# A hybrid DeltaNet and neighbourhood-attention layer: scores three gate tiles later, an empty step in the preparation, scan loads in another order

## The chip, the cores and the metric

The kernel runs on one NeuronCore of a Trainium2 chip. The core has a matrix engine (TensorE, PE in the profile; its weight loads are shown as PEld), a vector engine (VectorE, DVE), a scalar engine (ScalarE, ACT), GpSimd (POOL), and SyncE (SP), whose queue issues nearly all transfers between HBM and the on-chip memory SBUF. TensorE writes its sums into banks of PSUM, from which the others copy. The metric is the time of one execution on the device, in microseconds (us), as the median of several runs.

## What is computed

One layer on 1024 latent tokens of width 1024 with 256 context tokens ahead of them, so 1280 in all, in 32-bit floats. Cut to what matters here:

```
px = modulate(rms_norm(x), sh1, sc1) @ w_in          # and the same for the context
group A (4 heads of 128), forward and backward, chunk by chunk:
    q, k, v = silu(short_conv(...)); q, k normalised; decay g, gate beta
    m    = strict_lower((k*beta) k^T * decay);  u, w = solve(1 + m, ...)
    v_new = u - w S;  o = (q e^g) S + (q k^T * decay) v_new;  S = S e^g_last + k_dec^T v_new
    o = rms_norm(o_forward + o_backward) * silu(z)
group B (8 heads of 64): softmax over an 8 x 16 window of a 16 x 64 grid and all context keys
x = x + g1 * (concat(A, B) @ w_out)
x = x + g2 * swiglu(modulate(rms_norm(x), sh2, sc2))
```

The two directions of group A scan ten chunks of 128 tokens each: two of context, eight of latents. The solve is done by blocks of 32, all of it before the scans, since it doesn't depend on the state S.

## The kernel before

All matrix products are made from a high and a low part of each operand (three products for one), with sums in PSUM.

**Projection jobs.** A list of jobs runs over the columns of `w_in`: blocks k0 to k3, z1 (one half of the gate z), nk0 to nk3 with nv0 among them, q0 to q3, nq0 to nq3, v0, nv1, v1 to v3, and z0, the other half of the gate. A block holds 128 columns and is computed in eight steps over the depth (L405); a wide job holds 256 columns and is computed in ten tiles of 128 tokens (nv0, nv1) or eight (z0; only latents), 24 matmuls to a tile (L595). The job nv1 is the one that the loop calls `values`. A job's weights are loaded, cast to a high part on ACT and subtracted to a low part on POOL while the job before it runs. For a wide job they come in two halves through one raw buffer, so the second half is asked for when the first has been split (L586 to L588). After a block of kind q, k or v comes its convolution on DVE (L457, L461); later its transposes (L527) and stores.

**Background.** A generator `bg` is advanced by one call after each of a block's eight steps and by two after each tile of a wide job. From job nk0 on it first makes the inverses of the 32 x 32 blocks, then the preparations; what is left is drained ahead of v3. Another (`bg2`) makes the modulation.

**Preparation.** Ten preparations, each for a forward and a backward chunk at once. Each is a generator of seven calls: (1) decay terms on POOL, copies to `fx` on ACT; (2) decay matmuls (L967, L968), exponent on ACT, the mask product of `kk` on DVE (L974), the block inverses into `y` on POOL (L977), `at` on DVE; (3) block products `kk` x `fx` (L986) and their copy (L989); (4 to 6) three rounds of products (L997), each copied into `y` by DVE (forward, L999) and ACT (backward, L1000); (7) the end, which puts the stores of `y` on a list. Stores of `y` and `at` are issued on SP one or two calls later (L1009). Two preparations may be alive; a second starts once the first has had three calls. `y` has two buffers, used in turn, and the products two PSUM banks. Preparations 2 to 9 wait until the jobs of kind q are finished, which is at job nq2.

**Value windows.** After nv1's tiles the program asks SP for 64 copies inside HBM (L1107), which lay the values out by window (`vw_d`).

**Attention.** Group B is a generator (`fill`) that is advanced between other work. Its first call, ahead of v3's matmuls, asks for the first queries, keys, biases and values (L260 to L283). There are 32 blocks of two heads each; a block takes two calls: scores (L303), the softmax on DVE and ACT (L305 to L309), transposes (L314) with copies (L317), the product with the values (L324). In z0 it is called after each of the eight tiles. The rest is called beside the scans, `PACE` times to each call of a scan generator, and what is left after them.

**Scans.** `scan(d, c)` does one chunk of one direction in four calls (three in each direction's first chunk, which has no state): state times `kT` (L1195), state times `qT` (L1205), `y` times the residual (L1214), `at` times the new values (L1226), `kt` times the decayed values into the next state (L1231). `load(d, c, near)` asks SP for a chunk's tiles (all at L1164), for the next chunk while one is scanned. A chunk that the other direction needs next is loaded once.

The order of instructions on an engine starts from the order of the program, but a planner at build time moves instructions whose operands it expects later behind others; so order on PE and SP need not be the program's. The first part of the kernel, up to job k1, is excepted from it.

Of the kernel before, what the change touches and what calls it, by code (L numbers as in the profile page):

```python
# [51 lines left out]
NCONST = 4 * 128 + 4 * 32  # L52
WIN = (256, 0)
CTX = {256: slice(0, 256), 0: slice(384, 640)}
PACE = 0.63
AHEAD = {(1, 0): (3,), (1, 1): (3, 4), (2, 0): (4, 5), (2, 1): (5, 6, 7), (3, 0): (6, 7)}
ORDER = [list(range(NCH)), [1, 0] + list(range(9, 1, -1))]

# [30 lines left out]
def hybrid(ctx, tc, a, dbg):  # L89
# [50 lines left out]
    v_d = dram.tile([T, 512], F32, name="v_d", tag="v_d")  # L140
# [34 lines left out]
    bg = Background()  # L175
# [199 lines left out]
    with ExitStack() as bs:  # L375
# [541 lines left out]
        def preps():  # L917

            first_half.close()
            with ExitStack() as gs:  # L920
                pk = pools(gs, "pk", "left")
                shift(gs, "ppad", "left", 64)
                pp = pools(gs, "pp", "left")

                def work(name, bufs=2, dt=F32):
                    return (pk if name == "kk" else pp).tile([128, 4, 128], dt, name=name, tag=name, bufs=bufs)

                fxs = [work(f"fx{d}", 1) for d in range(2)]
                ys = [[work(f"y{d}{i}", 1) for d in range(2)] for i in range(2)]
                for t in fxs + ys[0] + ys[1]:  # L930
                    pool.memset(t, 0.0)
                q32 = [slice(b * 32, b * 32 + 32) for b in range(4)]

                def fetch(i):

                    got = []
                    for d in range(2):
                        c = ORDER[d][i]
                        kk, xc = work("kk", 6), pp.tile([128, 2, 4, 32], F32, name="xc", tag="xc", bufs=4)
                        sp.dma_start(kk, kk_d[:, c])  # L940
                        sp.dma_start(xc, x_d[:, d, :, c * 4:c * 4 + 4])
                        at = None
                        if c >= 2:
                            at = work("at", 4)
                            sp.dma_start(at, qk_d[:, c - 2])
                        got.append((d, c, kk, xc, at))
                    return i, got

                def prep(i, got):
                    y = ys[i % 2]  # L950
                    rgs = []
                    for d, c, kk, xc, at in got:
                        mle = M[C_LE + d].rearrange("p (o i) -> p o i", o=1).to_broadcast([128, 4, 128])
                        for gg in (GH, GL):
                            rg = work("rg", 4, F32R)
                            g = gg.bitcast(F32)[:, d, c].rearrange("p (h o) -> p h o", o=1).to_broadcast([128, 4, 128])
                            pool.tensor_tensor(rg, g, mle, OP.mult)
                            rgs.append(rg)
                    for d, c, kk, xc, at in got:
                        for q in q32:  # L960
                            act.copy(fxs[d][q, :, q], xc[q, 1])
                    yield 1
                    es = []
                    for d, c, kk, xc, at in got:
                        p = bank("pr")
                        for j in range(2):
                            pe.matmul(p, mr[:, d], fl(rgs[2 * d + j]), start=j == 0, stop=False)  # L967
                        pe.matmul(p, mr[:, 4], mneg[:, d].rearrange("p (o i) -> p o i", o=1).to_broadcast(  # L968
                            [128, 4, 128]), start=False, stop=True)
                        e = work("e", 2)  # L970
                        act.activation(fl(e), p, AF.Exp)
                        es.append(e)
                    for (d, c, kk, xc, at), e in zip(got, es):
                        dve.tensor_tensor(kk, kk, e, OP.mult)  # L974
                    for (d, c, kk, xc, at), e in zip(got, es):
                        for q in q32:
                            pool.tensor_copy(y[d][q, :, q], xc[q, 0])  # L977
                        if at is not None:
                            dve.tensor_tensor(at, at, e, OP.mult)
                            stores.append((at_d[d, c - 2], at, tick[0] + 2))  # L980
                    yield 1
                    ps = []
                    for d, c, kk, xc, at in got:
                        p = bank("pr")
                        for h in range(4):
                            pe.matmul(p[:, hs[h]], kk[:, h], fxs[d][:, h], start=True, stop=True)  # L986
                        ps.append(p)
                    for (d, c, kk, xc, at), p in zip(got, ps):
                        act.copy(fl(kk), p)  # L989
                    yield 1  # L990
                    for n in range(1, 4):
                        blk = (q32[3 - n], q32[n])
                        cols = (slice(128 - 32 * n, 128), slice(0, 32 * n))
                        ps = [bank("pr").rearrange("p (h i) -> p h i", h=4) for _ in got]
                        for h in range(4):
                            for (d, c, kk, xc, at), p in zip(got, ps):
                                pe.matmul(p[blk[d], h, :32 * n], kk[:, h, blk[d]], y[d][:, h, cols[d]],  # L997
                                          start=True, stop=True)
                        dve.tensor_copy(y[0][blk[0], :, cols[0]], ps[0][blk[0], :, :32 * n])  # L999
                        act.copy(y[1][blk[1], :, cols[1]], ps[1][blk[1], :, :32 * n])  # L1000
                        yield 1
                    for d, c, kk, xc, at in got:
                        stores.append((y_d[d, c], y[d], tick[0] + 1))

                stores, tick = [], [0]

                def flush(n):
                    while stores and stores[0][2] <= n:
                        sp.dma_start(*stores.pop(0)[:2])  # L1009

                todo = list(range(NCH))
                live, landing = [], []
                while live or todo or landing:
                    if not landing and todo and (todo[0] < 2 or all(x in done for x in queries)):
                        landing.append(fetch(todo.pop(0)))
                    if landing and (not live or len(live) < 2 and live[0][1] >= 3):
                        live.append([prep(*landing.pop(0)), 0])
                    if not live:
                        yield
                    for g in list(live):  # L1020
                        tick[0] += 1
                        flush(tick[0])
                        g[1] += 1
                        if not next(g[0], 0):
                            live.remove(g)
                        yield
                flush(tick[0] + 2)
# [23 lines left out]
        for n in range(2, len(jobs) + 2):  # L1051
# [24 lines left out]
            if isinstance(j, Wide):  # L1076
                for t, _ in enumerate(j.tiles()):
                    if t > 1 or not final:
                        next(fin, 0)
                    if final:  # L1080
                        next(fill)
                    if t == 4 and nrm:
                        nrm.norm()
                        for _ in fin:
                            pass
                        fin = nrm.finish()
                        done.add(n - 1)
                        nrm = None
                    bg.step(2)
            elif j:  # L1090
                for k in range(KT):
                    j.mm([k])
                    if k >= 3:
                        next(fin, 0)
                    bg.step(1)
                    if n > inv + 4:
                        bg2.step(1)
                j.evac()
# [42 lines left out]
    with ExitStack() as gs:  # L1141
# [18 lines left out]
        def load(d, c, near):  # L1160
# [6 lines left out]
            both = shared.pop(c, None)  # L1167
            if both is None:
                r = slice(c * 128, (c + 1) * 128)
                both = [tile_of("kT", fl(kT_d[:, c])), tile_of("v", v_d[r])]  # L1170
                both += [tile_of("kt", k_d[r]), tile_of("qT", fl(qT_d[:, c - 2])) if c >= 2 else None]
                if c in near:
                    shared[c] = both
            y = tile_of("y", fl(y_d[d, c]))
            at = tile_of("at", fl(at_d[d, c - 2])) if c >= 2 else None
            kT, v, kt, qT = both
            ready[d, c] = kT, qT, kt, v, y, at

        seen = set()
# [595 lines left out]
```

## Time and profile before

| | us |
|---|---|
| median of 3 runs | 1557.04 |
| lowest and highest | 1555.83, 1560.87 |
| the profiled execution | 1556.61 |
| its span (first to last instruction) | 1554.8 |
| PE busy in it | 1486.3 |
| job nv1 to v3 in it (about) | 447 to 556 |
| job z0 | to 607 |
| scans with attention beside them | 607 to 840 |
| output projection | to 923 |
| feed-forward part | from 923 |

The profile is of one execution. A view of busy time by stretches gives, for a start and an end in us from the span's start, how long each engine worked in it (with the number of its instructions), the clock that was granted to TensorE as a share of full speed, the busy share of the DMA engines and the rate. The view in order of time gives start, duration, engine, source line, operation, the tile written and the tiles read, and the number of such instructions merged into the row; in brackets stands how long the engine had been idle and what it had waited for. SPq rows are transfers being issued, with the time that issuing took. The view of waits gives the engine and line that waited, what it waited for, then us in total, times, and the longest one.

### The profile page before, as it was taken

Reading aid. Unit: us, or ns where it says so; the run is one execution under the profiler, and the core shown is the slowest. Engines: PE = TensorE matmul, PEld = TensorE weight load, DVE = VectorE, ACT = ScalarE, POOL = GpSimd, SP = SyncE. Lnnn points to the kernel's source line nnn. Section 1 sums busy time; section 2 is a strip of 40 time slices with the busy share of each in tenths; the row PEclk is TensorE's granted clock in tenths of the full one; section 3 lists DMA queues with packets and bytes.
Section 4 is the critical chain, followed back from the end, with each engine's and each line's share of the span. In section 5 each row is a group of like instructions: output and inputs, shape, how many; then the busy total and the mean of one; then the engine's idle time right before and its main releaser. Section 6 shows DMA issues by size and latency. Waiting matters only on the chain. (4 is left out here: it accounts for less than half of the span.)

```text
span 1554.8 us, 23965 instructions
## 1 busy us (share of the span) xinstructions
PE 1486.3 (96%) x8702; PEld 1239.4 (80%) x8702; DVE 993.5 (64%) x1712; ACT 727.8 (47%) x1404; POOL 234.1 (15%) x286
## 2 busy tenths in 40 slices
PE   6999999999899978999999999999999999999998
PEld 4788787677678858888887878888888888888887
DVE  5774496674454544667986559865666656689652
ACT  5442552535754336665874266333333334454440
POOL 1154500733625110111210000000000000000000
PEclk9999998899989979999999999999999999999999
DMA  9274221578545466888737601632222224698742
GB/s 388 62 222 126 72 75 55 163 228 241 191 145 183 137 186 193 298 275 265 241 101 246 228 34 59 225 107 105 102 102 102 103 101 156 228 376 290 243 143 82
DMA packets 204118, 267.35 MB, mean 172 GB/s; under 512 B 16736, under 2 KB 114528, under 8 KB 202976
## 3 DMA queue, kind: packets, MB, share of 16 engines
q1 hardware_dynamic: 198480, 261.07, 50.7%
q10 hardware_dynamic: 5520, 4.76, 0.9%
q8 instruction: 68, 1.11, 0.3%
q14 instruction: 50, 0.41, 0.1%
HBM read 201.02 MB, written 68.94 MB: 174 GB/s over the span
## 5 line engine op out<-in xcount | busy, mean ns | idle before, releaser
L405 PE MATMUL blk<-hh,whi 128*128 128x512 f32 (+1 forms) x410 | 124.3, 396 | 2.4 <-ACT kk L550 1.4
L1412 ACT CAST uhi<-wq 128x512 fp32r<-128x512 f32 x101 | 61.0, 622 | 131.9 <-issue 84.9
L1412 ACT CAST uhi<-ws 128x512 fp32r<-128x512 f32 x91 | 54.0, 621 | 146.4 <-PE ps L1351 96.5
L405 PE MATMUL blk<-hl,whi 128*128 128x512 f32 (+1 forms) x410 | 117.5, 379 | 0.3 <-DVE hl L707 0.3
L595 PE MATMUL blk<-zw,hh 128*128 128x256 f32 (+1 forms) x576 | 115.2, 294 | 0.9 <-ACT kk L550 0.8
L405 PE MATMUL blk<-hh,wlo 128*128 128x512 f32 (+1 forms) x410 | 115.1, 378 | 0.6 <-POOL wlo L200 0.6
L1413 DVE TENSOR_TENSOR ulo<-wq,uhi 128x512 fp32r<-128x512 f32 x101 | 67.6, 687 | 58.8 <-ACT uhi L1412 32.4
L1351 PE MATMUL ps<-hT,uhi 128*128 128x512 f32 x336 | 103.6, 390 | 0.0
L1351 PE MATMUL ps<-lT,uhi 128*128 128x512 f32 x336 | 103.5, 389 | 0.0
L1351 PE MATMUL ps<-hT,ulo 128*128 128x512 f32 x336 | 103.5, 389 | 0.0
L595 PEld LDWEIGHTS blk<-zw,hh 128*128 128x128 f32 x576 | 93.0, 193 | 4.7 <-issue 2.0
L1351 PE MATMUL ps<-hB,uhi 128*128 128x512 f32 x288 | 89.2, 391 | 0.6 <-ACT hB L1526 0.6
L1351 PE MATMUL ps<-lB,uhi 128*128 128x512 f32 x288 | 88.8, 389 | 0.4 <-DVE lB L1527 0.4
L1351 PE MATMUL ps<-hB,ulo 128*128 128x512 f32 x288 | 88.7, 389 | 0.0
L405 PEld LDWEIGHTS blk<-hh,wlo 128*128 128x128 f32 x410 | 72.7, 193 | 15.4 <-POOL wlo L200 0.9
L405 PEld LDWEIGHTS blk<-hh,whi 128*128 128x128 f32 x410 | 69.9, 194 | 18.6 <-issue 4.5
L405 PEld LDWEIGHTS blk<-hl,whi 128*128 128x128 f32 x410 | 72.9, 193 | 14.5 <-DVE hl L707 0.8
L595 PE MATMUL blk<-zw,hl 128*128 128x256 f32 (+1 forms) x288 | 83.5, 290 | 0.0
L1351 PEld LDWEIGHTS ps<-hT,ulo 128*128 128x128 f32 x336 | 63.1, 188 | 13.2
L1351 PEld LDWEIGHTS ps<-lT,uhi 128*128 128x128 f32 x336 | 63.1, 188 | 13.1
L1351 PEld LDWEIGHTS ps<-hT,uhi 128*128 128x128 f32 x336 | 62.9, 188 | 12.9
L200 POOL TENSOR_TENSOR wlo<-wraw,whi 128x1024 fp32r<-128x1024 f32 x18 | 45.3, 2517 | 180.6 <-ACT whi L199 173.2
(359 smaller groups left out, 3544.5 us busy)
## 6 DMA issues: line engine op xcount, KB each, us to landing
wq<-w_fo SPq DMA_DIRECT2D x99, 256.0 KB, 4.3
wq<-w_gu SPq DMA_DIRECT2D x88, 256.0 KB, 2.8
wad<-wa SPq DMA_DIRECT2D x64, 256.0 KB, 4.6
bt<-rpb SPq DMA_DIRECT2D x64, 192.0 KB, 3.5
t_d<-g SPq DMA_DIRECT2D x22, 512.0 KB, 3.6
fr<-t_d SPq DMA_DIRECT2D x44, 256.0 KB, 5.1
f_d<-g SPq DMA_DIRECT2D x33, 256.0 KB, 2.1
fr<-f_d SPq DMA_DIRECT2D x33, 256.0 KB, 4.1
```

The source lines that it names most:

```text
L200: lo_engine.tensor_tensor(o, r, h.bitcast(F32), OP.subtract)
L405: pe.matmul(o, ww[:, k], xx[k][:, s], start=k == 0 and j == 0, stop=k == KT - 1 and j == 2)
L595: pe.matmul(p[:, :c1 - c0], x[k][:, s], ww[:, k, c0:c1], start=k == 0 and j == 0, stop=k == KT - 1 and j == 2)
L1351: pe.matmul(o, w[wi][:, k], x[xi][:, k], start=first and k == 0 and j == 0, stop=k == n - 1 and j == 2, skip_group_check=True)
L1412: act.copy(hi, self.raw[key])
L1413: dve.tensor_tensor(lo, self.raw[key], hi.bitcast(F32), OP.subtract)
```

## The change

Six edits, none of which changes what is computed.

- The preparation has an empty call between calls 2 and 3, so it takes eight.
- A second preparation starts once the first has had four calls, not three.
- In nv1 the background is advanced by three calls a tile instead of two.
- In z0 the attention is not called after the first three tiles.
- `PACE` is 0.66 instead of 0.63.
- A chunk's loads are asked for in the order v, kt, y, kT, qT, at; before it was kT, v, kt, qT, y, at.

```
--- before.py
+++ after.py
@@ -52,7 +52,7 @@
 NCONST = 4 * 128 + 4 * 32
 WIN = (256, 0)
 CTX = {256: slice(0, 256), 0: slice(384, 640)}
-PACE = 0.63
+PACE = 0.66
 AHEAD = {(1, 0): (3,), (1, 1): (3, 4), (2, 0): (4, 5), (2, 1): (5, 6, 7), (3, 0): (6, 7)}
 ORDER = [list(range(NCH)), [1, 0] + list(range(9, 1, -1))]
 
@@ -979,6 +979,7 @@
                             dve.tensor_tensor(at, at, e, OP.mult)
                             stores.append((at_d[d, c - 2], at, tick[0] + 2))
                     yield 1
+                    yield 1
                     ps = []
                     for d, c, kk, xc, at in got:
                         p = bank("pr")
@@ -1013,7 +1014,7 @@
                 while live or todo or landing:
                     if not landing and todo and (todo[0] < 2 or all(x in done for x in queries)):
                         landing.append(fetch(todo.pop(0)))
-                    if landing and (not live or len(live) < 2 and live[0][1] >= 3):
+                    if landing and (not live or len(live) < 2 and live[0][1] >= 4):
                         live.append([prep(*landing.pop(0)), 0])
                     if not live:
                         yield
@@ -1077,7 +1078,7 @@
                 for t, _ in enumerate(j.tiles()):
                     if t > 1 or not final:
                         next(fin, 0)
-                    if final:
+                    if final and t > 2:
                         next(fill)
                     if t == 4 and nrm:
                         nrm.norm()
@@ -1086,7 +1087,7 @@
                         fin = nrm.finish()
                         done.add(n - 1)
                         nrm = None
-                    bg.step(2)
+                    bg.step(3 if n == values else 2)
             elif j:
                 for k in range(KT):
                     j.mm([k])
@@ -1167,13 +1168,15 @@
             both = shared.pop(c, None)
             if both is None:
                 r = slice(c * 128, (c + 1) * 128)
-                both = [tile_of("kT", fl(kT_d[:, c])), tile_of("v", v_d[r])]
-                both += [tile_of("kt", k_d[r]), tile_of("qT", fl(qT_d[:, c - 2])) if c >= 2 else None]
+                both = [tile_of("v", v_d[r]), tile_of("kt", k_d[r])]
+                y = tile_of("y", fl(y_d[d, c]))
+                both += [tile_of("kT", fl(kT_d[:, c])), tile_of("qT", fl(qT_d[:, c - 2])) if c >= 2 else None]
                 if c in near:
                     shared[c] = both
-            y = tile_of("y", fl(y_d[d, c]))
+            else:
+                y = tile_of("y", fl(y_d[d, c]))
             at = tile_of("at", fl(at_d[d, c - 2])) if c >= 2 else None
-            kT, v, kt, qT = both
+            v, kt, kT, qT = both
             ready[d, c] = kT, qT, kt, v, y, at
 
         seen = set()
```

More of the change, by code (lines that the diff above doesn't have):

```diff
@@ L54 @@
 CTX = {256: slice(0, 256), 0: slice(384, 640)}
-PACE = 0.63
+PACE = 0.66
 AHEAD = {(1, 0): (3,), (1, 1): (3, 4), (2, 0): (4, 5), (2, 1): (5, 6, 7), (3, 0): (6, 7)}
@@ L981, in prep @@
                     yield 1
+                    yield 1
                     ps = []
@@ L1015, in preps @@
                         landing.append(fetch(todo.pop(0)))
-                    if landing and (not live or len(live) < 2 and live[0][1] >= 3):
+                    if landing and (not live or len(live) < 2 and live[0][1] >= 4):
                         live.append([prep(*landing.pop(0)), 0])
@@ L1079, in hybrid @@
                         next(fin, 0)
-                    if final:
+                    if final and t > 2:
                         next(fill)
@@ L1088, in hybrid @@
                         nrm = None
-                    bg.step(2)
+                    bg.step(3 if n == values else 2)
             elif j:
@@ L1169, in load @@
                 r = slice(c * 128, (c + 1) * 128)
-                both = [tile_of("kT", fl(kT_d[:, c])), tile_of("v", v_d[r])]
-                both += [tile_of("kt", k_d[r]), tile_of("qT", fl(qT_d[:, c - 2])) if c >= 2 else None]
+                both = [tile_of("v", v_d[r]), tile_of("kt", k_d[r])]
+                y = tile_of("y", fl(y_d[d, c]))
+                both += [tile_of("kT", fl(kT_d[:, c])), tile_of("qT", fl(qT_d[:, c - 2])) if c >= 2 else None]
                 if c in near:
                     shared[c] = both
-            y = tile_of("y", fl(y_d[d, c]))
+            else:
+                y = tile_of("y", fl(y_d[d, c]))
             at = tile_of("at", fl(at_d[d, c - 2])) if c >= 2 else None
-            kT, v, kt, qT = both
+            v, kt, kT, qT = both
             ready[d, c] = kT, qT, kt, v, y, at
```

## The prediction

> **What bounds the kernel now.** I read the page's head first, then busy times over stretches chosen by stage, then the order of time around the worst stretch, engine by engine.
>
> ```profile
> span 1554.8 us, 23965 instructions
> PE 1486.3 (96%) x8702; PEld 1239.4 (80%) x8702; DVE 993.5 (64%) x1712; ACT 727.8 (47%) x1404; POOL 234.1 (15%) x286
> ```
>
> PE works 96% of the span, so only its pauses, and a clock below full speed after them, can be won. The stretches (start:end, length, then busy us and count of PE, PEld, DVE, ACT, POOL, then granted clock, DMA share, GB/s) show where those lie:
>
> ```profile
> 500.80:556.20 55.40, 54.87 (x361) 44.71 (x359) 29.25 (x37) 17.70 (x34) 11.79 (x16) 1.00 0.41 126
> 556.20:571.00 14.80, 4.21 (x20) 2.30 (x19) 10.64 (x17) 5.89 (x9) 1.07 (x4) 0.57 1.07 290
> 571.00:575.20 4.20, 4.06 (x19) 3.58 (x18) 2.98 (x6) 1.95 (x5) 2.31 (x2) 0.50 0.40 118
> 607.30:620.00 12.70, 9.47 (x75) 7.37 (x74) 5.69 (x12) 10.53 (x16) 2.01 (x4) 0.73 1.01 326
> 620.00:840.00 220.00, 213.85 (x1913) 186.29 (x1914) 164.76 (x495) 143.70 (x408) 33.27 (x65) 1.00 0.73 237
> 923.00:1341.00 418.00, 418.00 (x1852) 345.94 (x1851) 277.89 (x441) 169.00 (x298) 0.00 (x0) 1.00 0.34 116
> ```
>
> From 923 on PE never pauses, and the change touches nothing there. Between the last value projection (job v3, ended 556.2) and the z tiles (job z0) PE is idle 14.80 - 4.21 = 10.6 us. The 4.21 us it works run at 0.57 of the clock and lose 4.21 x 0.43 = 1.8; the next 4.06 run at 0.50 and lose 2.0. Together **14.4 us** go there. In order of time on PE:
>
> ```profile
> 555.58 0.75 PE L405 MATMUL blk<-hh,wlo 128*128 128x256 f32 x3
> 561.22 0.58 PE L303 MATMUL sc<-kh,qs 128*128 128x256 f16 x2 [4.90 <-DMA kh<-nk_d]
> 567.45 0.37 PE L303 MATMUL sc<-kh,qs 128*128 128x256 f16 x1 [3.60 <-DVE mx L305]
> 570.92 0.56 PE L595 MATMUL blk<-zw,hh 128*128 128x256 f32 x1
> ```
>
> The first scores stand ahead of z0's first tile, wait for their keys, then for the softmax. But they only stand where PE would have waited anyway: z0's weights (two halves through one buffer) were not there. Half 2, asked for last on SP, is cast and split only just then (engine rows SP, ACT, POOL):
>
> ```profile
> 504.43 25.95 SPq L1107 DMA_DIRECT2D vw_d<-nv_d  x40
> 534.03 1.96 SPq L1009 DMA_DIRECT2D y_d<-y  x2
> 536.09 0.61 SPq L586 DMA_DIRECT2D wraw<-w_z  x1
> 550.82 0.80 SPq L1009 DMA_DIRECT2D y_d<-y  x2
> 553.76 0.62 SPq L260 DMA_DIRECT2D qs<-nq_d  x1
> 563.61 0.60 SPq L586 DMA_DIRECT2D wraw<-w_z  x1
> 550.29 0.47 ACT L1000 COPY y<-pr 32x384 f32<-32x384 f32 x1 [1.00 <-PE pr L997]
> 550.78 1.05 ACT L587 CAST zw<-wraw 128x1024 fp32r<-128x1024 f32 x1
> 569.59 1.03 ACT L587 CAST zw<-wraw 128x1024 fp32r<-128x1024 f32 x1
> 570.70 2.37 POOL L588 TENSOR_TENSOR zw<-wraw,zw 128x1024 fp32r<-128x1024 f32 x1 [13.73 <-ACT zw L587]
> ```
>
> SP asks for 40 of the 64 value-window copies without a break until 530.4; stores of the preparation come behind them; the last y store is issued only at 550.8, with the attention's loads and the second half of z0's weights behind it. The last preparation is late for the same reason:
>
> ```profile
> 513.40 0.63 PE L967 MATMUL pr<-rg,mr 128*128 128x512 f32 x2
> 534.38 1.27 POOL L977 COPY y<-xc 32x128 f32<-32x128 f32 x4 [8.38 <-DMA y_d<-y]
> 544.45 0.44 PE L997 MATMUL pr<-y,kk 128*32 128x32 f32 x8
> ```
>
> Its decay matmuls ran at 513.4, but its y buffer is that of the preparation two before, whose y store is behind the copies; POOL waits for it, and the block products move from about 524 to 544.
>
> **The change part by part.**
>
> *Empty step, start at 4, three steps a tile.* No instruction is added. The preparation takes 8 calls instead of 7. Chunk pairs 2 to 9 (eight of them) start at job nq2; up to job v2 there are 8 + 8 + 8 + 20 + 8 + 8 = 60 calls, and 8 x 7 = 56 are used. After: 70 and 64, so nothing is left for the drain in either. What matters is the sixth of the eight, which owns the y buffer the last one needs. Two are alive and alternate: it ended at call 44, the last call of the value tiles (8 x 3 + 20), and its y stores were flushed at call 45, behind the 64 copies. Now it ends at call 51 of the 54 in that span (8 x 3 + 30), and its stores go ahead of the copies. So the last preparation is not held; its block products fall in v1 and v2, and its y stores follow the copies directly, at about 530.5 + 3 = 534 instead of 550.8. The attention's loads follow (ten of queries and keys, one of context values, three for the first block: 9.9 us from 553.76 to 563.61, so until about 544).
>
> z0's weights: half 1 asked for at about 536, as now; its cast at 550.78 stood behind the late y copies on ACT, which are gone. From request to the end of the split a half takes 570.70 + 2.37 - 563.61 = 9.5 us; two one after the other end at 536.1 + 19 = 555, against v3's end at 556.2. Bounds for what stays of the 14.4: nothing, or all of it and more (a rival). Slack is only 1 us, and a PE that arrives some us earlier does not make SP's copies earlier: I take **2.0 left**, so -12.4.
>
> *First scores three tiles later.* A z tile is 24 matmuls, from 496.50 to 499.45 about 2.9 us (first and last of one); a row of attention steps beside the scans is the last of these (only instructions on the scores' banks):
>
> ```profile
> 496.50 0.39 PE L595 MATMUL blk<-zw,hh 128*128 128x256 f32 x1
> 499.32 0.28 PE L595 MATMUL blk<-zw,hh 128*128 128x256 f32 x1
> 558.33 5.90 DVE L461 SCALAR_TENSOR_TENSOR cacc<-cr,cw,cacc 128x255 f32<-128x255 f32 x6
> 640.00:740.00 100.00, 55.43 (x510) 29.27 (x385) 20.75 (x26) 21.18 (x38) 0.00 (x0) 1.00 0.88 280
> ```
>
> Four tiles, 11.7 us, now lie ahead of the first scores: longer than v3's convolution keeps DVE (to 564.2), so keys, biases and DVE are there when scores come. Moved are three steps of 20 matmuls (40 to a block of two steps): 60 x 55.43 / 510 = 6.5 us of PE work, from z0 to the scans, which are PE's too (213.85 of 220). It costs **0** where PE works all the time; if it filled all 6.15 us of pauses from 620 to 840 it would gain that, and if nothing in the scans took it up it would cost 6.5 at the end.
>
> *PACE.* The attention needs 67 calls. Before: 1 + 8 in z0, so 58 beside the scans, reached at call 58 / 0.63, the 93rd of the scans' 96. After: 1 + 5, so 61 / 0.66, again the 93rd. The end is not moved: 0, inside the same bounds.
>
> *Preparation's own pauses.*
>
> ```profile
> PE pr L997 <- DVE y L999: 4.8, 3, 2.7
> PE pr L997 <- ACT kk L989: 3.5, 2, 2.9
> PE pr L986 <- DVE kk L974: 1.8, 3, 1.3
> PE pr L986 <- DVE y L999: 1.7, 2, 1.5
> 427.02 0.41 PE L997 MATMUL pr<-y,kk 128*32 128x32 f32 x8 [2.90 <-ACT kk L989]
> 459.77 1.07 PE L997 MATMUL pr<-y,kk 128*32 128x64 f32 x16 [2.69 <-DVE y L999]
> 420.00:440.00 20.00, 16.51 (x116) 13.14 (x117) 9.30 (x11) 12.45 (x23) 9.33 (x12) 0.91 0.45 145
> 460.00:480.00 20.00, 19.98 (x164) 17.74 (x161) 6.29 (x9) 8.97 (x22) 8.01 (x12) 0.85 0.55 168
> ```
>
> The empty step lies between DVE's mask (kk, L974) and its product (L986): it covers that wait, **-1.8**. The others are waits for copies after products, which get no step; they shift. Bounds: all four go, 11.8, and with them the slow clock behind the two long ones, 16.51 x 0.09 + 19.98 x 0.15 = 4.5: -16.3; or the ten added calls in the value tiles cost what the twenty did, (2.69 + 3.0) / 20 = 0.28 each: +2.8. I take -1.8, the row that the edit names.
>
> [...]
>
> *Loads of the scans.*
>
> ```profile
> 615.76 0.63 SPq L1164 DMA_DIRECT2D y<-y_d x1
> 620.73 1.13 PE L1214 MATMUL ps<-v,y 128*128 128x128 f32 x8 [1.33 <-DMA y<-y_d]
> ```
>
> The first scan step has no state and needs y and v, not kT. y is asked for third instead of fourth, one issue earlier: 0.4 to 0.6 us, which PE waits for (1.33). I take **-0.5**; bounds 0 and -1.3. In later chunks kT comes behind kt and y, whose buffers come free later: one or two issues, 0.6 to 1.3 us, if PE had no attention work between. It waits for no kT anywhere now, so 0; eight such chunks at 1.3 would be +10.
>
> **Sum**, against the profiled execution's 1556.6 (span 1554.8 and 1.8 around it; 0.4 under the median of 1557.04): 1556.6 - 12.4 - 1.8 - 0.5 = 1541.9, so **1542**.
>
> **The rivals.**
>
> *The weights stay late.* If the y stores still come behind the copies, or the first half's cast is again placed behind other ACT work, z0 cannot start before about 571. Then delaying the scores takes the only work out of the gap: 4.21 x 0.57 = 2.4 us more lost, less 2.3 of the small terms: 1556.7, the change doesn't do what it says. For it: the casts at 550.78 and 569.59. Against: the count of calls puts the stores ahead.
>
> *Half.* Weights come at about 562: 1542 + 6 = 1548.
>
> *The value tiles choke (slower).* In the value tiles three calls now share one tile of 2.9 us; a preparation passes from one stage to the next after two thirds of a tile. Where copy and sequencer don't fit, PE pauses as at 459.77, which costs 2.69 and 3.0 of slow clock, 5.7. The gain of 14.7 is used up from the third such tile; four of ten make 1542 + 23 = 1565. For it: there are only two banks for these products, and DVE is in the convolution of v0 at that time. Against: from 500.8 to 556.2, one call to a smaller piece, PE lost 0.5 us, and matmuls of the tile are put between products.
>
> *All pauses of the preparation go.* 1542 - 14.5 = 1527 at the bound; half of it 1535.
>
> **How the numbers follow.** Forecast 0.52 (its own range 1537 to 1546), half 0.12, pauses 0.12, weights late 0.12, choke 0.12. No change is within 0.3%, 4.7 us of 1557.0. Faster: 0.52 + 0.12 + 0.12 = 0.76; same: the late weights, 0.11; slower: the choke and a little of the late weights, 0.13. The range goes from 1533 (the pauses' half, 1535, with the first scan's 1.3) to 1557 (late weights), leaving out the choke and the far end of the pauses.
>
> **What would show it.** Right: first z tile within 3 us of v3's last matmul, first scores some four tiles on; y stores of the last preparation issued near 534; block products of all preparations done before 530; granted clock near 1 around that place; no wait of L986 for kk; scans ending on the same distance from z0's end plus 6 us. Wrong: PE idle ahead of L595 with the cast of zw as releaser; pauses of 2 us or more in several value tiles; waits of L1195 for kT.

## The result and the profile after

The changed kernel takes 1550.36 us, the median of 7 runs (1549.54 to 1553.73); the kernel before, run beside it, 1559.35 (also 7). The ratio of after to before is 0.996, with a 95% interval of 0.9946 to 0.9974: faster, by 6 us (4 to 8) by the ratio and 9 by the medians, where 15 were forecast. The profiled executions are 1549.54 and 1556.61, so 7.1 us are to be explained. Two executions among all those below, one of the kernel before (1877.8 us) and one of the preparation alone (2440.43), lie far above the rest, at granted clocks of 0.73 and 0.56; the ratios leave them out, and the medians move by less than 1 us without them. Lines after about 982 of the code are one to three further down: L986 is now L987, L997 L998, L999 and L1000 are L1000 and L1001, L1107 is L1108.

The head of the page of the kernel after:

```profile
span 1547.5 us, 23963 instructions
PE 1479.8 (96%) x8702; PEld 1235.2 (80%) x8702; DVE 994.3 (64%) x1712; ACT 727.7 (47%) x1404; POOL 233.6 (15%) x286
```

PE's busy time has fallen by 6.5 us with the same 8702 matmuls, while the mean granted clock went from 0.979 to 0.982: I read that as a faster clock, not as shorter waits. Busy times by stretches (columns as in the prediction) say where; first, of the kernel before, from the start of the preparations among the query jobs to the end of v3:

```profile
364.00:556.33 192.33, 180.83 (x1270) 148.06 (x1268) 91.62 (x116) 98.43 (x186) 75.37 (x95) 0.97 0.55 170
```

The same of the kernel after, then the gap up to z0 and the slow matmuls behind it:

```profile
364.00:548.50 184.50, 175.78 (x1275) 144.78 (x1274) 93.98 (x120) 97.46 (x185) 73.90 (x95) 1.00 0.57 177
548.50:563.40 14.90, 3.95 (x20) 2.26 (x19) 12.72 (x17) 6.66 (x10) 2.59 (x2) 0.63 1.06 294
563.40:568.00 4.60, 4.46 (x21) 3.98 (x20) 3.03 (x6) 2.01 (x5) 2.37 (x2) 0.50 0.34 104
```

The first stretch is 7.8 us shorter: PE's idle time went from 11.5 to 8.7 us (-2.8) and its busy time from 180.8 to 175.8 (-5.0), at a granted clock of 1.00 instead of 0.97. That is the whole gain in this pair of profiles. How it divides between idle time and clock differs from execution to execution: over the same stretch, from 364 to the end of v3, the clock is 0.97 to 1.00 in the profiles below that have the new preparation and 0.96 to 0.98 in those that have the old one (the kernels with copies on ACT apart). The gap, which was to bring 12.4 us, is there as before. Counted as in the prediction it costs 14.90 - 3.95 = 10.95 of idle time, 3.95 x 0.37 = 1.5 and 4.46 x 0.50 = 2.2 of slow clock, together 14.6 (14.4 before).

PE in order of time around the gap, kernel after:

```profile
547.75 0.75 PE L405 MATMUL blk<-hh,wlo 128*128 128x256 f32 x3
...
553.04 0.58 PE L303 MATMUL sc<-kh,qs 128*128 128x256 f16 x2 [4.54 <-DMA kh<-nk_d]
...
559.55 0.37 PE L303 MATMUL sc<-kh,qs 128*128 128x256 f16 x1 [4.11 <-DVE mx L305]
...
563.38 0.56 PE L595 MATMUL blk<-zw,hh 128*128 128x256 f32 x1
```

The program now calls the attention only after z0's fourth tile, yet on PE the first scores still stand ahead of z0's first matmul, with like waits: the planner put them there. What held z0 is seen on the other engines, the kernel after in order of time (SP, then ACT, then POOL):

```profile
533.18 2.42 SPq L1010 DMA_DIRECT2D y_d<-y  x4
535.68 0.61 SPq L586 DMA_DIRECT2D wraw<-w_z  x1
545.47 0.37 SPq L535 DMA_DIRECT2D v_d<-vt  x1
545.93 0.63 SPq L260 DMA_DIRECT2D qs<-nq_d  x1
...
555.34 0.60 SPq L586 DMA_DIRECT2D wraw<-w_z  x1
```

```profile
548.13 1.35 ACT L453 COPY cr<-blk 128x256 f32<-128x256 f32 x3 [5.77 <-PE blk L405]
549.35 1.07 ACT L587 CAST zw<-wraw 128x1024 fp32r<-128x1024 f32 x1
...
562.05 1.03 ACT L587 CAST zw<-wraw 128x1024 fp32r<-128x1024 f32 x1
```

```profile
563.15 2.37 POOL L588 TENSOR_TENSOR zw<-wraw,zw 128x1024 fp32r<-128x1024 f32 x1 [10.31 <-ACT zw L587]
```

The stores of y follow the copies at 533.18, as forecast. But half 1 of z0's weights, asked for at 535.68, is cast only at 549.35: in ACT's order the cast is behind v3's copies out of PSUM, for which ACT itself waits 5.77 us. And SP issues nothing between 536.3 and 545.5, where a store of values (v1's) is next in its order and waits for DVE, which only then has the values ready (the kernel after, waits of SP from 530 to 560):

```profile
SPq L535 <- DVE vt L531: 9.1, 1, 9.1
```

Behind that store come the attention's loads, and only then, at 555.34, half 2. Its split starts at 563.15, and z0 with it.

The pauses and the clock in the preparation, kernel after: waits of PE from 364 to 548 (us in total, times, longest), then two rows in order of time with the stretch around them, and the last product of the last preparation.

```profile
PE pr L987 <- ACT y L1001: 2.5, 1, 2.5
PE pr L987 <- ACT kk L990: 2.3, 1, 2.3
PE pr L998 <- ACT kk L990: 1.2, 2, 0.6
PE pr L987 <- DVE kk L974: 1.1, 2, 0.8
...
PE pr L987 <- DVE y L1000: 0.7, 1, 0.7
```

```profile
447.49 1.16 PE L987 MATMUL pr<-fx,kk 128*128 128x128 f32 x8 [2.54 <-ACT y L1001]
451.64 1.16 PE L987 MATMUL pr<-fx,kk 128*128 128x128 f32 x8 [2.29 <-ACT kk L990]
...
520.28 0.68 PE L998 MATMUL pr<-y,kk 128*32 128x96 f32 x10
```

```profile
440.00:460.00 20.00, 15.12 (x140) 13.46 (x139) 15.20 (x19) 15.87 (x29) 7.33 (x10) 1.00 0.59 184
```

The same view of the kernel before, from 364 to 556 (the rows that the prediction showed were of the whole span):

```profile
PE pr L997 <- ACT kk L989: 3.5, 2, 2.9
PE pr L997 <- DVE y L999: 2.9, 2, 2.7
PE pr L986 <- DVE kk L974: 1.8, 3, 1.3
PE pr L986 <- DVE y L999: 1.7, 2, 1.5
...
PE pr L997 <- ACT y L1000: 0.6, 2, 0.3
```

The preparation's pauses add up to 7.8 us where they were 10.5. The wait that the edit names, the product L987 for DVE's mask, is down from 1.8 to 1.1 only; the other 2.0 went from waits for the copies of kk and y. The last preparation is done by 521 instead of about 550. And two pauses of 2.54 and 2.29 us left the clock at 1.00.

### The profile page after: what moved, and what is told of

Read it like the earlier page. It is cut to its first block, busy times and chain, and to the rows that moved or that the text cites. A ratio compares the mean times of both kernels' runs of the same rounds, so it can differ in the third digit from the quotient of the medians.

```text
span 1547.5 us, 23963 instructions
## 1 busy us (share of the span) xinstructions
PE 1479.8 (96%) x8702; PEld 1235.2 (80%) x8702; DVE 994.3 (64%) x1712; ACT 727.7 (47%) x1404; POOL 233.6 (15%) x286
## 5 line engine op out<-in xcount | busy, mean ns | idle before, releaser
L595 PE MATMUL blk<-zw,hh 128*128 128x256 f32 (+1 forms) x576 | 115.0, 293 | 1.3 <-ACT kk L550 1.1
L595 PEld LDWEIGHTS blk<-zw,hh 128*128 128x128 f32 x576 | 92.8, 192 | 5.2 <-ACT kk L550 1.4
L595 PE MATMUL blk<-zw,hl 128*128 128x256 f32 (+1 forms) x288 | 83.2, 289 | 0.0
```

What stands on the lines that cost most here:

```text
L595: pe.matmul(p[:, :c1 - c0], x[k][:, s], ww[:, k, c0:c1], start=k == 0 and j == 0, stop=k == KT - 1 and j == 2)
```

## The experiments

All times are medians, ratios are to the kernel before as it was run beside each (its medians were 1559.35, 1558.14, 1558.6 and 1557.46 us), with 95% intervals. "Gap" is from the end of v3's last matmul to the first of z0, in the profile of that run. One profile is one execution, and executions of a kernel differ by up to 14 us (the kernel before from 1549.68 to 1563.29), so gaps and waits are read from profiles and worths from the medians. Part of that spread shows in the stretch from 260 to 364: its clock is 0.98 in the profiles of "after, two calls" and "before, half of the copies later" and 0.90 to 0.94 in the others (those with copies on ACT apart), whatever the edits. PE got through 568 and 574 matmuls there in those two and 538 to 553 in the others, so v3 ends earlier in those two for that reason too.

| kernel | median | ratio | gap |
|---|---|---|---|
| before | 1559.35 | 1 | 14.6 |
| after | 1550.36 | 0.996 [0.9946, 0.9974] | 14.9 |
| preparation alone | 1550.32 | 0.9955 [0.9934, 0.9975] | 15.1 |
| the rest alone | 1556.15 | 0.9989 [0.9968, 1.001] | 15.7 |
| three calls alone | 1558.79 | 1.0016 [0.9998, 1.0034] | 12.7 |
| after, two calls | 1548.28 | 0.9953 [0.9933, 0.9972] | 17.0 |
| after, copies on ACT | 1554.77 | 0.9985 [0.9969, 1.0] | 1.0 |
| before, copies on ACT | 1566.99 | 1.0057 [1.0035, 1.008] | 1.0 |
| after, half of the copies later | **1538.05** | 0.9874 [0.9851, 0.9897] | 1.0 |
| the same, early scores | 1541.14 | 0.9894 [0.987, 0.9919] | 1.0 |
| the same, old preparation | 1543.74 | 0.9914 [0.9895, 0.9934] | 1.0 |
| after, casts on POOL, weights first | 1544.79 | 0.9918 [0.9899, 0.9937] | 6.2 |
| after, a quarter first | 1538.34 | 0.9886 [0.9863, 0.9909] | 1.0 |
| before, half of the copies later | 1543.73 | 0.9919 [0.9895, 0.9944] | 1.0 |

### Which edits carry the gain

The preparation's three edits alone, in the kernel before:

```
                     yield 1
+                    yield 1
                     ps = []
...
-                    if landing and (not live or len(live) < 2 and live[0][1] >= 3):
+                    if landing and (not live or len(live) < 2 and live[0][1] >= 4):
...
-                    bg.step(2)
+                    bg.step(3 if n == values else 2)
```

> The kernel before with the preparation's three edits alone (empty call, start at four, three calls a value tile). Theory A (all that was won lies in the preparation: pauses of 9.9 us become 7.6, slow clock of 4.9 us behind two of them goes): ratio to before 0.995 to 0.997, about 1551 to 1554, z0's first tile still some 14 to 15 us after v3's last matmul. Rival B (late scores, PACE or the loads carry half of it): ratio 0.998 or nearer to 1.

The kernel after with these three undone, so only late scores, `PACE` and the order of loads:

> The kernel before with late scores, PACE 0.66 and the new order of loads alone. Theory A: no change, ratio 0.999 to 1.001, gap ahead of z0 14 to 15 us. Rival B: ratio 0.998 or less.

Measured: 0.9955 and 0.9989. The preparation's edits are the whole effect; the rest can't be told from nothing. Both have the gap, at 15.1 and 15.7 us.

Of the three, the three calls a tile in nv1 were tried by themselves in the kernel before, and taken out of the kernel after:

```
# three calls alone, in before
-                    bg.step(2)
+                    bg.step(3 if n == values else 2)
```

> The kernel before with three calls a value tile alone. Theory J (the empty call and the later start win the preparation's 7 us; three calls only make room for them): ratio to before 0.999 to 1.002. Rival K (three calls carry it, as they take the last preparations off v1 and v2): 0.995 to 0.997.

```
# two calls, in after
-                    bg.step(3 if n == values else 2)
+                    bg.step(2)
```

> The changed kernel with two calls a value tile as before: the last preparation's last four calls are drained ahead of v3. Theory J: 0.995 to 0.998, as the pauses ahead of the value tiles are those that go. Rival K: 1.000 or slower, with the last products and y stores later than in the changed kernel and the gap ahead of z0 longer.

Three calls alone gain nothing (1.0016), and without them the gain is all there (0.9953). So the empty call and the later start of the second preparation carry it. The waits of PE from 364 to 538 in the kernel after with two calls:

```profile
PE pr L987 <- ACT y L1001: 2.8, 1, 2.8
PE pr L998 <- ACT kk L990: 1.2, 2, 0.6
PE pr L987 <- DVE kk L974: 1.1, 2, 0.8
```

The mask's wait is the same 1.1; the waits of products for the copies of y and kk are what is shorter than before. The empty call and the later start were not tried apart from each other.

### What holds z0

The theory was that the 64 copies, issued one after the other on SP, delay all that z0 and the attention need. To test it, they were issued from ACT instead:

```
-                            sp.dma_start(vw_d[r * 32:r * 32 + 32, :, cb, ch],
-                                         vlat[4 * ch + r, ...])
+                            act.dma_start(vw_d[r * 32:r * 32 + 32, :, cb, ch],
+                                          vlat[4 * ch + r, ...])
```

In the kernel after:

> The changed kernel with the 64 value-window copies issued from ACT's queue instead of SP's. Theory C (z0's weights hold the gap, and they are late because the copies hold SP): z0's first tile within 4 us of v3's last matmul, 10 to 12 us won over the changed kernel, 1538 to 1541, ratio to before 0.987 to 0.989. Rival D (the gap is set by queries and keys or by the buffers, not by SP's copies): gap of 10 us or more, ratio 0.995 to 0.997. Rival E (64 issues of 0.33 us on ACT, 21 us, hold its copies and PE pauses in v1 to v3): gap closed but as much lost ahead of it, 1548 to 1556.

In the kernel before:

> The kernel before with only the copies moved to ACT's queue. Theory C: gap closed to 4 us or less here too, without any edit of the change: 1545 to 1549, ratio 0.991 to 0.993. Rival D: ratio 0.999 to 1.001. Rival E: 1555 or more.

In both the gap closed, and the time went elsewhere. Order of time on ACT's queue, ACT and PE, kernel after with copies on ACT:

```profile
500.37 28.48 ACTq L1108 DMA_DIRECT2D vw_d<-nv_d  x43
528.89 0.36 ACT L1001 COPY y<-pr 32x256 f32<-32x256 f32 x1 [28.82 <-DMA vw_d<-nv_d]
529.39 1.19 PE L967 MATMUL pr<-rg,mr 128*128 128x512 f32 x2 [13.76 <-ACT y L1001]
```

For 28.5 us ACT issued 43 copies and did nothing else; PE ran out of work behind ACT's copy of y and stood for 13.76 us, which is the gap's price at another place. In the kernel before the like pause was 11.2 us, and the kernel was slower by 0.57%. The closed gap alone proves little here, since v3 ended later by itself (at 566.4 instead of 548.5 in the kernel after). But half 2 of z0's weights was asked for at 543.47 instead of 555.34, and its split began at 550.15 instead of 563.15, so the weights did come earlier. The cleaner test follows; ACT, at any rate, is no free place for the copies.

So the copies were left on SP and half of them (two of the four column blocks of latents) moved behind z0's loads:

```
+        def windows(cbs):
+            for cb in cbs:
+                for ch in range(4):
+                    for r in range(4):
+                        sp.dma_start(vw_d[r * 32:r * 32 + 32, :, cb, ch], vlat[4 * ch + r, ...])
...
             if n + 1 < len(jobs):
                 jobs[n + 1].prefetch()
+            if n == len(jobs) - 2:
+                windows((2, 3))
...
             if isinstance(j, Wide) and n == values:
-                for cb in range(4):
...
+                windows((0, 1))
```

> The changed kernel with 32 of the 64 value-window copies (column blocks 2 and 3) asked for on SP only behind the loads of z0's weights, the other 32 as before. Theory C (the copies on SP hold z0's weights, and these the gap): z0's first tile within 4 us of v3's last matmul, 10 to 12 us less than the changed kernel, 1537 to 1541, ratio to before 0.987 to 0.990. Rival D (the gap has another holder, such as the casts' place on ACT): a gap of 8 us or more, 1548 to 1551. Rival F (the late copies hold the attention's loads or its value windows, and PE pauses there instead): gap closed, but 5 us or more of new waits of L303 or L324 in z0, 1545 to 1550.

Measured 1538.05, 0.9874: 12.3 us faster than the changed kernel by the medians (13 by the ratios), and the fastest of the study. Its order of time on PE, SP and ACT, and the stretch around the former gap:

```profile
553.92 0.38 PE L595 MATMUL blk<-zw,hh 128*128 128x256 f32 x1 [1.03 <-ACT cr L453]
...
566.69 0.27 PE L303 MATMUL sc<-kh,qs 128*128 128x256 f16 x1
```

```profile
522.92 0.61 SPq L586 DMA_DIRECT2D wraw<-w_z  x1
...
531.99 0.60 SPq L586 DMA_DIRECT2D wraw<-w_z  x1
...
544.12 16.84 SPq L1059 DMA_DIRECT2D vw_d<-nv_d  x25
```

```profile
527.91 1.05 ACT L587 CAST zw<-wraw 128x1024 fp32r<-128x1024 f32 x1 [3.57 <-DMA wraw<-w_z]
...
536.08 1.04 ACT L587 CAST zw<-wraw 128x1024 fp32r<-128x1024 f32 x1 [1.73 <-DMA wraw<-w_z]
...
552.52 1.35 ACT L453 COPY cr<-blk 128x256 f32<-128x256 f32 x3 [3.95 <-PE blk L405]
```

```profile
548.00:575.00 27.00, 25.95 (x200) 24.20 (x199) 14.67 (x27) 10.11 (x19) 0.00 (x0) 1.00 0.56 165
```

Both halves are asked for and cast 16 us and more before v3's copies. z0 starts 1.03 us after v3, the clock stays at 1.00, and only now do the first scores run after four z tiles, 566.69 - 553.92 = 12.8 us on, without waiting. The later copies lie where SP has nothing urgent.

Three variants tell its parts apart. With the scores called from z0's first tile again (`if final:` and `PACE` 0.63):

> As e5, but with first scores after the first z tile and PACE 0.63 as before the change. Theory G (once the weights come in time, the three tiles without scores are worth what they were meant for: keys, biases and DVE are late by some us): 2 to 5 us more than e5, with PE waiting at L303 for keys or for DVE. Rival H (late scores are worth nothing in either case): within 1 us of e5.

It starts z0 as early, and its first scores do not wait either:

```profile
554.50 0.28 PE L303 MATMUL sc<-kh,qs 128*128 128x256 f16 x1
```

1541.14 against 1538.05, with intervals that overlap: by the medians, whether the late scores are worth up to 3 us or nothing stays open. The profiles point to some worth: PE's waits from 590 to 660, where the scans start, add up to 7.7 us here and to 3.8 in the kernel with late scores (the largest here is 3.1, for y). In the three kernels that follow they are 4.1 and 2.8 with late scores and 6.8 with early ones. Each is one execution.

With the preparation of before (the three edits undone):

> As e5, but with the preparation as before the change (seven calls, start at three, two calls a value tile). Theory C with the preparation's gain by itself (7 us, in pauses and slow clock between 394 and 501): 6 to 8 us more than e5, 1544 to 1548, gap closed too. Rival I (the preparation's edits are needed to close the gap, as the last y store comes late without them): gap of 5 us or more and 12 us or more above e5.

1543.74, with a gap of 1.03: the preparation gains 5.7 us here too (the two intervals barely touch), by itself and not through the gap.

With only a quarter of the copies first (`windows((0,))`, then `windows((1, 2, 3))`):

> As e5, but only 16 of the 64 copies (column block 0) ahead of z0's weights, 48 behind. Theory C: the gap is closed already in e5 (1.0 us, PSUM copies), so no more than 1 us from e5: 1536 to 1540. Rival F (48 late copies hold the windows of column blocks 1 to 3): PE waits of 2 us or more at L324 in z0, 1540 to 1546.

1538.34, like the half: once z0's weights are in time, more room on SP brings nothing.

And the split alone in the kernel before, with none of the change:

> The kernel before, with none of the change's edits, only 32 of the 64 copies asked for behind z0's weights. Theory C: gap of 4 us or less, 10 to 13 us less than before, ratio 0.991 to 0.994. Rival I (without the change's preparation the last y stores are too late): gap of 8 us or more, ratio 0.997 or more.

1543.73, and 0.9919 of 1557.46 is 12.6 us less (8.7 to 16.4 by the interval): that is what the split alone gains. PE in order of time there:

```profile
548.08 0.75 PE L405 MATMUL blk<-hh,wlo 128*128 128x256 f32 x3
...
549.86 0.38 PE L595 MATMUL blk<-zw,hh 128*128 128x256 f32 x1 [1.03 <-ACT cr L453]
```

The gap closes without any part of the change. And z0's first tile comes first as soon as its weights are early, though this kernel calls the scores from that tile on.

The last test kept the copies and removed the two other things that stood ahead of z0's weights: the attention's first loads were put behind z0's, and z0's casts from ACT to POOL:

```
                 jobs[n + 1].room()
-                fill = attention(pools(attn, "nw", "left", 2))
-                next(fill)
...
                 jobs[n + 1].prefetch()
+            if n == len(jobs) - 2:
+                fill = attention(pools(attn, "nw", "left", 2))
+                next(fill)
...
-                    act.copy(self.hi[:, :, s], r)
+                    if self.lasting:
+                        pool.tensor_copy(self.hi[:, :, s], r)
+                    else:
+                        act.copy(self.hi[:, :, s], r)
```

> The changed kernel with all copies as they are, but z0's weights asked for ahead of the attention's first loads in the program and cast on POOL instead of ACT. Theory C': with the copies in place the weights' second half is asked for at about 549 to 551 and is there at about 560: gap of 8 to 12 us, 1546 to 1549. Rival D (the casts' place on ACT and the loads' order are all that holds the gap): gap of 4 us or less, 1538 to 1541.

1544.79, 5.6 us under the changed kernel by the medians: between the two cases that were expected. Order of time on POOL, SP and PE:

```profile
540.35 1.54 POOL L588 CAST zw<-wraw 128x1024 fp32r<-128x1024 f32 x1 [1.09 <-DMA wraw<-w_z]
```

```profile
545.39 0.37 SPq L535 DMA_DIRECT2D v_d<-vt  x1
...
547.82 0.59 SPq L586 DMA_DIRECT2D wraw<-w_z  x1
```

```profile
554.64 0.58 PE L598 MATMUL blk<-zw,hh 128*128 128x256 f32 x1 [6.21 <-POOL zw L588]
```

Half 1, asked for at 535.62, was in SBUF by 540.35. In the changed kernel, which asked for it at the same time, it must then have lain there for 9 us until ACT's order came to its cast. With POOL in ACT's place half 2 still went out only at 547.82, behind the store of values at 545.39, so 6.2 of the 14.9 us of the gap stay. Both the cast's place on ACT and SP's order hold z0, then; how the 8.7 us that went divide between this kernel's two edits was not tried apart. Earlier loads remove all of it.

## Why the prediction was half right

**What bounds the kernel** was read rightly: PE's pauses and the slow clock after them, the largest of them the 14.4 us ahead of z0, held by z0's weights and these by SP's copies. Closing it is worth about what the sum said: 12.4 predicted, 12.6 measured with the split in the kernel before. Two readings on the way were a little off, without weight in the sum. "From 923 on PE never pauses" holds to 1341; of the 213.8 us behind that PE worked 209.57. And the z tile's last row ends at 499.32 + 0.28 = 499.60, not 499.45.

**The step that failed** is the one from the early y stores to early weights, the term of -12.4, which came to nothing: 14.6 us are still lost there. Its first half came true: y stores at 533.18 against 534, block products done by 521. Its second half said that the cast "stood behind the late y copies on ACT, which are gone" and that the two halves run "one after the other" in 19 us from 536.1. The late y copies were only what happened to be ahead of the cast in the old order. With them gone, the cast took its place behind the next late thing on ACT, v3's PSUM copies, at 549.35 instead of 550.78; the sum had counted on about 542 (asked for at 536.1, and 6.0 us from request to cast as in half 2 of before, 563.61 to 569.59). The same on SP: the attention's loads were to end "about 544", and started at 545.93, behind the store of v1's values, for which SP waited 9.1 us. That store stood in the same place in the kernel before, between the last y store and the loads, in a row that the prediction did not show:

```profile
553.29 0.37 SPq L535 DMA_DIRECT2D v_d<-vt  x1
```

The prediction had traced each wait to what stood ahead of it, and did not ask what was next in that queue. It had named the danger, as the rival in which "the first half's cast is again placed behind other ACT work", and had given it 0.12. Its two terms also took from each other: with v3 ending at 548.5 by the faster preparation, weights at the forecast 555 would still have left a gap of 6.5 us, not 2.0. Why the planner gives the cast and the store those places was not measured; that the cast and the loads come earlier when the weights' first half is asked for some 13 us earlier is shown by the split.

**Late scores at 0.** "Four tiles, 11.7 us, now lie ahead of the first scores" did not come about in the changed kernel, since the planner kept them in the gap; it did in the kernel with half of the copies later (12.8 us, no wait). The cost of 0 was not measured in the change itself; in the kernels with the gap closed the profiles lean to a gain, and the medians, 3 us apart, can't tell it from none.

**Preparation at -1.8.** Right in sign, too small in size: the profiles show -7.8, the preparation alone 1558.14 - 1550.32 = 7.8 by medians (7.0 by the ratio). The row "that the edit names" gave 0.7 of it. The others were said to "shift", and 2.0 us of them went. The larger part in this pair of profiles, 5.0, is the clock: what the prediction had put into the bound of -16.3 and not into the value taken. The choke in the value tiles did not come: three calls a tile cost nothing.

**Loads at -0.5.** No gain is left: PE's waits for y at the start of the scans are, in the kernel after,

```profile
PE ps L1217 <- DMA y<-y_d: 2.3, 2, 1.6
```

against one of 1.33 before. The wait that the prediction named did shrink, to 0.66 at 607.16, but a second one of 1.60 follows at 610.54. In the median the loads, late scores and `PACE` together are 0.9989 [0.9968, 1.001].

**The cases.** The outcome is two rivals at once: the weights stay late (1556.7, of which 1.8 for the preparation) and half of the preparation's bound. With 7.8 for 1.8, the former gives 1550.7, and 1550.36 was measured. That it fits so closely is luck: this rival also books 2.4 us for a gap without work, though the scores stayed in it, and takes off 0.5 for the loads, which were not won. The two concern different stretches and neither excludes the other; the prediction gave each a chance only with everything else as forecast, so their sum had no chance of its own. The range held it, since it reached to the late weights.

## What to carry to other kernels

When a change takes away what a stalled instruction waited behind, list what is next ahead of it on the same queue, with its time, before booking the gain; here a cast moved by 1.4 us where almost 9 were counted on. Bulk transfers that are needed late should be issued behind those that are needed soon; here cutting a run of 64 in two was worth more than the whole change. A clock that is a few hundredths under full speed over a long stretch is a term of its own in the sum (0.97 instead of 1.00 over some 190 us: 5 us in this pair of profiles), and cases that concern different stretches should be combined rather than only listed.

## What the runs showed of the hardware

**Pauses and the clock.** In the kernel before, pauses of 2.90 and 2.69 us came with a granted clock of 0.91 and 0.85 in the 20 us around or behind them; in the kernel after, pauses of 2.54 and 2.29 us left it at 1.00 from 440 to 460. Length alone does not decide it: in the kernel with half of the copies later, pauses of 2.39 and 2.44 us, at 448.81 and 453.11, were followed by a slow clock:

```profile
453.11 1.16 PE L987 MATMUL pr<-fx,kk 128*128 128x128 f32 x8 [2.44 <-ACT kk L990]
452.00:460.00 8.00, 6.89 (x54) 6.13 (x55) 4.58 (x7) 6.69 (x15) 3.76 (x8) 0.79 0.58 180
```

Single matmuls of a wide job in it (L595, 128x256) took 0.41 us at 454.84 and 455.06, and 0.28 again at 458.57. In the kernel with casts on POOL, pauses of 2.61 and 2.25 us, at 447.44 and 451.55, left the clock at 1.00 from 364 to 500. What else decides stays open. In the gap of the kernel after, with pauses of 4.54 and 4.11 us, the clock was 0.63 and then 0.50.

**Issuing has a price on the engine that issues.** 43 copies inside HBM took ACT 28.48 us, 0.66 each, and on SP 4 of them took 2.52, 0.63 each, while the store of values took 0.37. On SP that time held up what was next on its queue; on ACT it also stopped the copies out of PSUM (28.82 us of waiting) and, through them, PE (13.76 us).
